# A two-layer hybrid decoder trunk: one more Strassen-Winograd step in each gate/up group, with block sums and raw weights in four shared slots

## The chip, the cores and the metric

The kernel runs on one core of a Trainium2 chip. The metric is the device time of one execution in microseconds (us). PE is the matrix engine (PEld its weight loads), DVE the vector engine, ACT the scalar engine, POOL the GpSimd engine and SP the engine whose queue issues the weight loads. Each engine works through its own list of instructions, fixed when the program is built; semaphores order the engines among each other.

## The reference

256 tokens of width 2048 pass through two layers, in float32. Layer 0 mixes tokens by trailing means over 2, 4, 8 and 16 tokens and a 512x512 product per channel group; layer 1 by differential attention with 8 heads. A SwiGLU network with 5632 hidden columns stands behind each mixer.

```python
def swiglu(h, wg, wu, wd):
    return (jax.nn.silu(h @ wg) * (h @ wu)) @ wd

for i in range(DEPTH):                       # DEPTH = 2
    hn = rmsnorm(h, norm_mix[i])
    mix = pool_mixer(...) if i == 0 else diff_attention(...)
    h = h + mix
    h = h + swiglu(rmsnorm(h, norm_ffn[i]), w_gate[i], w_up[i], w_down[i])
return rmsnorm(h, final_norm)
```

## The kernel before, in words

**Float32 through three products.** Every operand is kept as two parts of the matrix engine's 32-bit format: a rounded `hi` and the rest `lo`. A product is hi·hi + hi·lo + lo·hi, three matmuls of 128x128 by 128x512. For the weights this means, for each 1 MB tile `raw` of 128x(4x512) that SP's queue loads: ACT casts it to `whi` (line 115), and DVE subtracts, `wlo = raw - whi` (line 116).

**Groups and steps.** `group` computes four 128x512 results (two token blocks by two column blocks) as a sum over eight steps, one for each pair of input chunks (six steps in the down products of the last chunk). In the network of a layer, a gate/up group holds the gate columns on the left and the up columns on the right; there are eleven, in `CHUNKS` of 4, 4 and 3, and each chunk is followed by two down products (`o` = 0, 1) that read the chunk's hidden tiles `h`.

**Two kinds of step.** A plain step makes eight block products, 24 matmuls, and needs whi and wlo of all four blocks of `raw` (128x2048). A step "by sevens" multiplies the 2x2 blocks in the Strassen-Winograd way: seven products, 21 matmuls. For that DVE first forms four block sums `tsum` of the raw weights (`sums`: one instruction of 128x1024 in line 121, two of 128x512 in lines 123 and 124), ACT casts them to `thi` (line 130) and DVE forms `tlo = tsum - thi` (line 131); of the raw blocks only three are needed in halves (128x1536). `SEVEN` lists the steps of a gate/up group that go by sevens, `SEVEN_DOWN` those of a down product. `tsum`, `thi` and `tlo` have one buffer each, `raw`, `whi` and `wlo` three each.

**The end of a group.** `combined` (lines 195 to 212) turns the seven accumulators, each in a PSUM bank of its own, and the plain steps' results into the four results: two copies on ACT and eight additions on DVE (lines 202 to 211). Behind a gate/up group come silu on ACT (line 463), the product with up on DVE (line 464), and `pair`: transposes on PE into PSUM, and the halves of the hidden tile, with the block differences where the down step goes by sevens (lines 247 to 268).

**What sets the order.** A scheduler lists the instructions of each engine when the program is built; each engine keeps to its list on the chip. SP's queue issues the loads in order, each when its `raw` buffer is free.

Of the kernel before, what the change touches and what calls it, by code (L numbers as in the profile page):

```python
# [9 lines left out]
F32 = mybir.dt.float32  # L10
F32R = mybir.dt.float32r
AF = mybir.ActivationFunctionType
ALU = mybir.AluOpType
# [25 lines left out]

SEVEN = (2, 4, 6)  # L40
SEVEN_DOWN = (2, 4, 6)
# [11 lines left out]
def trunk_kernel(ctx, tc, x_n, gains, scale_in, final_in, subln, lam_in, band, dist,  # L53
# [21 lines left out]
    def bank(i, shape=(P, 512)):  # L75
        return psum.tile(list(shape), F32, name=f"b{i}", tag=f"b{i}")


    def aux(shape=(P, 512)):
# [5 lines left out]
    dist_sb = const.tile([P, 2 * P], F32, name="dist_sb")  # L85
    ident = const.tile([P, P], F32, name="ident")
    ones = const.tile([P, P], F32, name="ones")
    nc.vector.memset(ones, 1.0)
    make_identity(nc, ident)

    x_tok = resid.tile([P, 2, D], F32, name="x_tok")
# [26 lines left out]

    def sums(pool, raw):
        t = pool.tile([P, 4, 512], F32, name="tsum")  # L120
        nc.vector.tensor_tensor(t[:, T1:T3 + 1], raw[:, B11:B22 + 1],  # L121
                                raw[:, B12:B12 + 1].broadcast_to([P, 2, 512]), ALU.add)
        nc.vector.tensor_tensor(t[:, T2], t[:, T1], raw[:, B22], ALU.add)  # L123
        nc.vector.tensor_tensor(t[:, T4], t[:, T2], raw[:, B21], ALU.add)  # L124
        return t
# [12 lines left out]
    def group(steps, pool, by_bank=0):  # L138


        plan = []
        for a, seven, src in steps:
            if seven:
                plan.append([(M1, [(A11, 0, B11)]), (M2, [(A12, 0, B21)]), (M6, [(S2, 1, T2)]), (M7, [(S3, 1, T3)]),
                             (P5, [(S1, 1, T1)]), (P3, [(S4, 0, B22)]), (P4, [(A22, 1, T4)])])
            else:
                plan.append([(C11, [((0, 0), 0, B11), ((1, 0), 0, B21)]), (C12, [((0, 0), 0, B12), ((1, 0), 0, B22)]),
                             (C21, [((0, 1), 0, B11), ((1, 1), 0, B21)]), (C22, [((0, 1), 0, B12), ((1, 1), 0, B22)])])
        left = {}
# [3 lines left out]
        ps = {}  # L153

        def prepared(seven, src):
            raw = load(src)
            t = sums(pool, raw) if seven else None
            w = [halves(raw, B11 if seven else 0)]
            if seven:
                w.append(sum_halves(pool, t))  # L160
            return w

        def products(a, seven, w, b, parts):
            first = b not in ps
            if first:
                ps[b] = bank(b)
            for at, which, block in parts:
                hi, lo = w[which]
                if seven:
                    ah, al = a[:, 0, at], a[:, 1, at]  # L170
                else:
                    k, t = at
                    if a.shape[2] == 8:
                        slot = ((A11, A21), (A12, A22))[k][t]
                        ah, al = a[:, 0, slot], a[:, 1, slot]
                    else:
                        ah, al = (a[:, k, i, t * P:(t + 1) * P] for i in range(2))
                for x, y in ((ah, hi), (ah, lo), (al, hi)):
                    left[b] -= 1
                    nc.tensor.matmul(ps[b], x, y[:, block], start=first, stop=(left[b] == 0))  # L180
# [12 lines left out]
        return ps  # L193

    def combined(ps, pool):


        if M1 not in ps:
            return [[ps[C11], ps[C12]], [ps[C21], ps[C22]]]
        m1, u2, u3, p5 = (pool.tile([P, 512], F32, name=f"c{i}") for i in ("11", "12", "21", "22"))  # L200
# [6 lines left out]
        nc.vector.tensor_tensor(p5, p5, u3, ALU.subtract)  # L207
        nc.vector.tensor_tensor(u2, ps[P3], u2, ALU.add)
# [35 lines left out]

    def pair(dst, src, gains, seven):

        ps = aux((P, 2, 2, P))
        for i in range(2):
# [31 lines left out]
    with tc.tile_pool(name="start", bufs=1, reuse_waits="tile") as st:  # L280

        warm = tmp.tile([P, 8], F32, name="warm", bufs=1)
        nc.scalar.activation(warm[:, 0:1], ones[:, 0:1], AF.Sqrt)
# [4 lines left out]
        w_pool = [st.tile([P, 4, 512], F32, name=f"w{g}") for g in range(PLAIN)]  # L288
        scale_sb = st.tile([P, D], F32, name="scale_sb")
# [17 lines left out]
        load_x(1)  # L307
        nc.sync.dma_start(out=w_pool[1], in_=pool_w[1])
        w_pool.append(load(pool_w[2]))
# [22 lines left out]
        def product(g, some):  # L332

            if some[0] == 0:
                yp[g] = [bank(4 + 2 * (g % 2) + t) for t in range(2)]
                if g >= PLAIN:
                    w_pool[g] = halves(w_pool[g])
# [75 lines left out]
    turn["of"] = 4  # L413
    nc.sync.dma_start(out=dist_sb, in_=dist)

    def finish(cs, ys, final_sb, ss):

        for t in range(2):
            part = tmp.tile([P, 64], F32, name="part", bufs=2)
            nc.vector.tensor_reduce(part[:, 0:1], ss[:, t, 0:2], AX.X, ALU.add)  # L420
# [22 lines left out]
    def ffn(layer, xq, ss, next_op, next_gain):  # L443
# [3 lines left out]
        with tc.tile_pool(name=f"ffn{layer}", bufs=1, reuse_waits="tile") as hp:  # L447
            g0 = 0
            ys = []
            for c, n in enumerate(CHUNKS):  # L450
# [6 lines left out]
                for g in range(g0, g0 + n):  # L457

                    by_seven = SEVEN[-1:] if g == 0 and layer == 0 else SEVEN
                    cs = combined(group([(xq[p], p in by_seven, w_gu[layer][g, p]) for p in range(NP)], hp), hp)  # L460
# [4 lines left out]
                    for i in range(2):  # L465
                        at = 2 * (g - g0) + i
                        ht = hp.tile(pair_shape(at in SEVEN_DOWN), F32R, name="h", tag=f"h{at}")
                        pair(ht, lambda k, t: cs[t][1][:, (2 * i + k) * P:(2 * i + k + 1) * P], None, at in SEVEN_DOWN)
                        hp_tiles.append(ht)
                for o in range(2):  # L470
# [13 lines left out]
                    for b, t in ((0, 0), (0, 1), (1, 0), (1, 1)):  # L484
# [5 lines left out]
                        if last and next_op is None:  # L490
                            if b == 0 and t == 0:
                                ys.append([hp.tile([P, 2, 2, 512], F32, name="y", tag=("tsum", "thi")[i]) for i in range(2)])
                                ys = ys[0]
# [12 lines left out]
    with tc.tile_pool(name="attn", bufs=1, reuse_waits="tile") as ap_, ExitStack() as heads:  # L506
# [86 lines left out]
        for g in range(2):  # L593
            cs = scaled(combined(group([(xp[p], p in SEVEN_QKV, w_v[g, p]) for p in range(NP)], op_), op_), (r_col, r_col))
            for h in range(4 * g, 4 * g + 4):
# [11 lines left out]
                for t in range(2):  # L607
                    nc.scalar.activation(on[:, t, :], op[:, t, :], AF.Copy, scale=ro[:, t:t + 1])
                oT[h] = op_.tile(pair_shape(h in SEVEN_O), F32R, name=f"oT{h}")
                pair(oT[h], lambda i, t: on[:, t, i * P:(i + 1) * P], [gs[:, i:i + 1] for i in range(2)], h in SEVEN_O)  # L610
# [98 lines left out]
```

## Time and profile before

| | us |
|---|---|
| median of the runs | 1845.46 (1845.2 to 1845.46) |
| profiled execution, its own time | 1846.21 |
| its span, first to last instruction | 1844.4 |
| PE busy | 1829.2 (99%) |
| PEld busy | 1495.6 (81%) |
| DVE busy | 1604.2 (87%) |
| ACT busy | 1038.0 (56%) |
| granted PE clock | 0.997 |

An engine is busy from the start to the end of an instruction, and instructions of one engine overlap at their edges, so the step from start to start is shorter than the duration of one. PE's matmuls overlap far more: one lasts 392 ns by its row, and the next starts about 227 ns after it.

### The profile page before, as it was taken

How to read it: one execution, taken by the hardware profiler on the slowest of the kernel's cores; microseconds unless marked ns; L12 is line 12 of the kernel's file. 1: busy time of each engine (PE TensorE's matmuls, PEld its weight loads, DVE VectorE, ACT ScalarE, POOL GpSimd, SP SyncE). 2: the span in 40 equal slices, each digit the busy share in tenths (PEclk: the TensorE clock that was granted, in tenths of full speed). 3: DMA queues.
4: the chain of work that ended last, by engine and by line, in shares of the span. 5: the costliest groups of instructions: out<-in, count | busy, mean ns of one | idle time of the engine just before them, and what ended most of it. 6: DMA issues, size and time to landing. Idle time of an engine off the chain costs nothing.

```text
span 1844.4 us, 20901 instructions
## 1 busy us (share of the span) xinstructions
PE 1829.2 (99%) x8210; PEld 1495.6 (81%) x8210; DVE 1604.2 (87%) x1662; ACT 1038.0 (56%) x1006; POOL 0.7 (0%) x6
## 2 busy tenths in 40 slices
PE   9999999999999999999999999999999999999998
PEld 6788888888888888888888888788888888888886
DVE  6889998898989899988888678998989899998986
ACT  6555555555554556665566655555555555545553
POOL 0000000000000000000000000000000000000000
PEclk9999999999999999999999999999999999999999
DMA  7555555655555555555454454555555555565552
GB/s 273 183 201 187 193 210 194 210 196 194 203 198 204 202 186 183 208 180 171 173 177 164 160 188 176 205 203 187 204 205 204 188 201 183 206 227 204 206 186 111
DMA packets 50642, 356.80 MB, mean 193 GB/s; under 512 B 6000, under 2 KB 6128, under 8 KB 8048
## 3 DMA queue, kind: packets, MB, share of 16 engines
q1 hardware_dynamic: 49824, 353.85, 54.4%
q10 hardware_dynamic: 720, 1.62, 0.2%
q8 instruction: 64, 1.05, 0.2%
q14 instruction: 34, 0.28, 0.0%
HBM read 353.36 MB, written 2.10 MB: 193 GB/s over the span
## 4 chain that ended last, share of the span: by engine, by line
PE 95%; DVE 2%; ACT 1%; issue 1%; DMA 1%; SPq 0%; DVEq 0%; ACTq 0%
PE b L180 90%; PE b L250 2%; PE b L342 1%; DVE wlo L116 1%; PE b L554 1%; PE b L345 1%; PE b L584 0%; DMA w<-pool_w 0%; DMA raw<-w_gu 0%; DVE tlo L131 0%; ACT whi L115 0%; DVE tsum L121 0%; PE b L600 0%; PE b L598 0%; PE b L599 0%
## 5 line engine op out<-in xcount | busy, mean ns | idle before, releaser
L115 ACT CAST whi<-raw 128x1536 fp32r<-128x1536 f32 (+1 forms) x330 | 585.2, 1774 | 585.4 <-PE b L180 499.6
L180 PE MATMUL b<-whi,xp 128*128 128x512 f32 x2824 | 908.8, 392 | 1.2 <-DVE c L203 1.0
L116 DVE TENSOR_TENSOR wlo<-raw,whi 128x1536 fp32r<-128x1536 f32 (+1 forms) x330 | 697.3, 2113 | 193.1 <-ACT whi L115 192.9
L180 PEld LDWEIGHTS b<-whi,xp 128*128 128x128 f32 x2824 | 528.3, 188 | 110.1 <-DVE c L203 1.5
L180 PE MATMUL b<-wlo,xp 128*128 128x512 f32 x1412 | 551.8, 391 | 1.6 <-DVE wlo L116 1.6
L180 PE MATMUL b<-whi,h 128*128 128x512 f32 x1108 | 354.5, 390 | 0.0
L180 PEld LDWEIGHTS b<-wlo,xp 128*128 128x128 f32 x1412 | 265.3, 188 | 55.5 <-DVE wlo L116 1.9
L131 DVE TENSOR_TENSOR tlo<-tsum,thi 128x2048 fp32r<-128x2048 f32 x108 | 246.7, 2285 | 3.9 <-ACT thi L130 3.9
L180 PEld LDWEIGHTS b<-whi,h 128*128 128x128 f32 x1108 | 207.5, 188 | 43.1
L180 PE MATMUL b<-wlo,h 128*128 128x512 f32 x554 | 215.8, 389 | 0.0
L130 ACT CAST thi<-tsum 128x2048 fp32r<-128x2048 f32 x108 | 206.3, 1910 | 13.7 <-DVE tsum L124 13.6
L180 PE MATMUL b<-thi,xp 128*128 128x512 f32 x608 | 211.8, 390 | 0.0
L121 DVE TENSOR_TENSOR tsum<-raw 128x1024 f32<-128x1024 f32 x108 | 131.8, 1220 | 2.3 <-DMA raw<-w_v 0.6
L180 PEld LDWEIGHTS b<-thi,xp 128*128 128x128 f32 x608 | 113.9, 188 | 24.0 <-ACT thi L130 0.9
L180 PEld LDWEIGHTS b<-wlo,h 128*128 128x128 f32 x554 | 104.0, 188 | 21.3
L180 PE MATMUL b<-tlo,xp 128*128 128x512 f32 x304 | 119.5, 393 | 0.0
L180 PE MATMUL b<-thi,h 128*128 128x512 f32 x240 | 83.7, 389 | 0.0
L124 DVE TENSOR_TENSOR tsum<-tsum,raw 128x512 f32<-128x512 f32 x108 | 74.3, 688 | 2.3
L123 DVE TENSOR_TENSOR tsum<-tsum,raw 128x512 f32<-128x512 f32 x108 | 73.9, 684 | 0.6
L180 PE MATMUL b<-whi,oT 128*128 128x512 f32 x236 | 74.4, 392 | 0.0
L180 PEld LDWEIGHTS b<-tlo,xp 128*128 128x128 f32 x304 | 57.0, 188 | 16.1 <-DVE tlo L131 4.4
L180 PEld LDWEIGHTS b<-thi,h 128*128 128x128 f32 x240 | 45.1, 188 | 9.2
(147 smaller groups left out, 1192.5 us busy)
## 6 DMA issues: line engine op xcount, KB each, us to landing
raw<-w_gu SPq DMA_DIRECT2D x176, 1024.0 KB, 4.9
raw<-w_down SPq DMA_DIRECT2D x88, 1024.0 KB, 4.8
raw<-w_qk SPq DMA_DIRECT2D x32, 1024.0 KB, 4.9
raw<-w_v SPq DMA_DIRECT2D x16, 1024.0 KB, 4.8
raw<-w_o SPq DMA_DIRECT2D x16, 1024.0 KB, 4.8
raw<-pool_w SPq DMA_DIRECT2D x2, 1024.0 KB, 13.8
x_tok<-x_n SPq DMA_DIRECT2D x2, 768.0 KB, 9.0
w<-pool_w SPq DMA_DIRECT2D x2, 512.0 KB, 6.6
```

Source lines behind the costliest of these rows:

```text
L115: nc.scalar.copy(hi[:, lo_block:], raw[:, lo_block:])
L116: nc.vector.tensor_tensor(lo[:, lo_block:], raw[:, lo_block:], f32(hi[:, lo_block:]), ALU.subtract)
L121: nc.vector.tensor_tensor(t[:, T1:T3 + 1], raw[:, B11:B22 + 1], raw[:, B12:B12 + 1].broadcast_to([P, 2, 512]), ALU.add)
L123: nc.vector.tensor_tensor(t[:, T2], t[:, T1], raw[:, B22], ALU.add)
L124: nc.vector.tensor_tensor(t[:, T4], t[:, T2], raw[:, B21], ALU.add)
L130: nc.scalar.copy(hi, t)
L131: nc.vector.tensor_tensor(lo, t, f32(hi), ALU.subtract)
L180: nc.tensor.matmul(ps[b], x, y[:, block], start=first, stop=(left[b] == 0))
L250: nc.tensor.transpose(ps[:, i, 1 - t if seven else t], src(i, t), ident)
L342: nc.tensor.matmul(yp[g][t], a[:, rows], w[:, at], start=(at == 0), stop=(at == 3))
L345: nc.tensor.matmul(yp[g][t], u, v[:, at], start=(at == 0 and j == 0), stop=(at == 3 and j == 2))
L554: nc.tensor.matmul(sc[:, :nk], qk[:, 0, c, qb * P:(qb + 1) * P], qk[:, 1, c, :nk], start=True, stop=True)
```

## The change

- **`SEVEN` goes from (2, 4, 6) to (0, 2, 4, 6).** The first gate/up group of layer 0 keeps only step 6 by sevens, and that of layer 1 keeps (2, 4, 6); the other ten of each layer have four steps by sevens, and so four plain ones. The attention products and the down products keep their lists.
- **Buffers.** `raw` and `tsum` share one ring of four buffers; before, `raw` had three and `tsum` one of its own. A buffer is handed on in the order of the program, four allocations later.
- **`group`.** The products of a step by sevens are issued in another order: those on raw weights first, those on sums behind. P3 and P4 sit in two neighbouring banks that are allocated together.
- **`combined`.** Two subtractions become one instruction over 2x512 columns, and so do the two additions that read P3 and P4 (lines 211 and 212 of the changed kernel). Six DVE instructions where eight were.
- **`pair` of the hidden tiles** transposes into bank X instead of a rotating one. Small tiles (`ones`, `dist_sb`, `part`, the attention outputs of heads 4 to 7) move to other pools.

```diff
-SEVEN = (2, 4, 6)
+SEVEN = (0, 2, 4, 6)
...
-    wraw = ctx.enter_context(tc.tile_pool(name="wraw", bufs=3))
+    wraw = ctx.enter_context(tc.tile_pool(name="wraw", bufs=4))
...
-        raw = wraw.tile([P, 4, 512], F32, name="raw")
+        raw = wraw.tile([P, 4, 512], F32, name="raw", tag="raw")
...
-        t = pool.tile([P, 4, 512], F32, name="tsum")
+        t = wraw.tile([P, 4, 512], F32, name="tsum", tag="raw")
...
-                plan.append([(M1, [(A11, 0, B11)]), (M2, [(A12, 0, B21)]), (M6, [(S2, 1, T2)]), (M7, [(S3, 1, T3)]),
-                             (P5, [(S1, 1, T1)]), (P3, [(S4, 0, B22)]), (P4, [(A22, 1, T4)])])
+                raw = [(M1, [(A11, 0, B11)]), (M2, [(A12, 0, B21)]), (P3, [(S4, 0, B22)])]
+                summed = [(P5, [(S1, 1, T1)]), (M7, [(S3, 1, T3)]), (M6, [(S2, 1, T2)]), (P4, [(A22, 1, T4)])]
+                late = 3 if plan else 2
+                plan.append(raw[:late] + summed[:3] + raw[late:] + summed[3:])
...
-        nc.vector.tensor_tensor(u2, p5, u2, ALU.subtract)
-        nc.vector.tensor_tensor(p5, p5, u3, ALU.subtract)
-        nc.vector.tensor_tensor(u2, ps[P3], u2, ALU.add)
-        nc.vector.tensor_tensor(u3, ps[P4], u3, ALU.add)
+        nc.vector.tensor_tensor(c[:, 1:4:2], c[:, 3:4].broadcast_to([P, 2, 512]), c[:, 1:3], ALU.subtract)
+        nc.vector.tensor_tensor(c[:, 1:3], ps["both"], c[:, 1:3], ALU.add)
...
-                    by_seven = SEVEN[-1:] if g == 0 and layer == 0 else SEVEN
+                    by_seven = SEVEN if g else SEVEN[1:] if layer else SEVEN[-1:]
...
-                        pair(ht, lambda k, t: cs[t][1][:, (2 * i + k) * P:(2 * i + k + 1) * P], None, at in SEVEN_DOWN)
+                        pair(ht, lambda k, t: cs[t][1][:, (2 * i + k) * P:(2 * i + k + 1) * P], None, at in SEVEN_DOWN, X)
```

DVE in the middle of a gate/up group, before (a step by sevens from its sums to `tlo`, and the plain step's `wlo` between them):

```order
L121 TENSOR_TENSOR tsum<-raw 128x1024
L116 TENSOR_TENSOR wlo<-raw,whi 128x1536
L123 TENSOR_TENSOR tsum<-tsum,raw 128x512
L124 TENSOR_TENSOR tsum<-tsum,raw 128x512
L116 TENSOR_TENSOR wlo<-raw,whi 128x2048
L131 TENSOR_TENSOR tlo<-tsum,thi 128x2048
```

The same place now, for steps 4 and 5 of a group:

```order
L120 TENSOR_TENSOR tsum<-raw 128x1024
L115 TENSOR_TENSOR wlo<-raw,whi 128x1536
L122 TENSOR_TENSOR tsum<-tsum,raw 128x512
L123 TENSOR_TENSOR tsum<-tsum,raw 128x512
L130 TENSOR_TENSOR tlo<-tsum,thi 128x2048
L115 TENSOR_TENSOR wlo<-raw,whi 128x2048
```

The plain step's `wlo` (128x2048) stood between the last sum and `tlo`; now it stands behind `tlo`, and nothing stands between. So it is at 28 places in each layer's network from its first combination to that of its eleventh group; before at none of them.

DVE at the end of a gate/up group, before (lines 202 to 211 are the combination, 464 the product with up; 116 belongs to the next group's plain first steps and 121, 123 to its step 2):

```order
L202 TENSOR_TENSOR c_9573<-b_9394,c_9572 128x512
L121 TENSOR_TENSOR tsum<-raw 128x1024
L204 TENSOR_TENSOR c_9574<-b_9398,c_9573 128x512
L203 TENSOR_TENSOR c_9572<-b_9315,c_9572 128x512
L206 TENSOR_TENSOR c_9573<-c_9575,c_9573 128x512
L116 TENSOR_TENSOR wlo<-raw,whi 128x2048
L207 TENSOR_TENSOR c_9575<-c_9575,c_9574 128x512
L208 TENSOR_TENSOR c_9573<-b_9322,c_9573 128x512
L209 TENSOR_TENSOR c_9574<-b_9329,c_9574 128x512
L211 TENSOR_TENSOR c_9575<-b_9336,c_9575 128x512
L464 SCALAR_TENSOR_TENSOR c_9573<-c_9573,r_tok,c_9572 128x512
L464 SCALAR_TENSOR_TENSOR c_9575<-c_9575,r_tok,c_9574 128x512
```

And now (120, 122, 123 are sums of the next group's step 0, 115 and 130 its `wlo` and `tlo`):

```order
L122 TENSOR_TENSOR tsum<-tsum,raw 128x512
L211 TENSOR_TENSOR c<-c 128x2x512
L123 TENSOR_TENSOR tsum<-tsum,raw 128x512
L212 TENSOR_TENSOR c<-b_2880,c 128x1024
L214 TENSOR_TENSOR c<-b_2911,c 128x512
L470 SCALAR_TENSOR_TENSOR c<-c,r_tok 128x512
L115 TENSOR_TENSOR wlo<-raw,whi 128x1536
L470 SCALAR_TENSOR_TENSOR c<-c,r_tok 128x512
L130 TENSOR_TENSOR tlo<-tsum,thi 128x2048
```

The next group's first step needed one `wlo`, which stood ahead of the combination's end; now it needs three sums, `wlo` and `tlo`, and both halves stand behind the combination's last addition.

PE at that boundary, before (b_9618 to b_9632 are the next group's banks, line 250 the transposes of the hidden tile):

```order
L180 MATMUL b_9618<-whi,xp 128x512
L180 MATMUL b_9618<-wlo,xp 128x512
L180 MATMUL b_9618<-whi,xp 128x512 x2
L180 MATMUL b_9618<-wlo,xp 128x512
L180 MATMUL b_9618<-whi,xp 128x512
L180 MATMUL b_9625<-whi,xp 128x512
```

And now:

```order
L184 MATMUL b_3166<-whi,xp 128x512
L184 MATMUL b_3182<-whi,xp 128x512
L184 MATMUL b_3170<-thi,xp 128x512
L184 MATMUL b_3174<-thi,xp 128x512
L184 MATMUL b_3178<-thi,xp 128x512
L253 MATMUL b_3127<-ident,c 128x128
L184 MATMUL b_3162<-wlo,xp 128x512
```

Where eighteen matmuls on whole products ran first, five matmuls on hi parts now stand ahead of the transposes and of the first that needs `wlo`.

More of the change, by code (lines that the diff above doesn't have):

```diff
@@ L76, in bank, with two_banks @@
         return psum.tile(list(shape), F32, name=f"b{i}", tag=f"b{i}")
+    def two_banks():
+        both = psum.tile([P, 2, 512], F32, name="b45", tag="b45")
+        return [both[:, i] for i in range(2)], both
     def aux(shape=(P, 512)):
@@ L117, in halves, with sums @@
         return hi, lo
-    def sums(pool, raw):
-        t = pool.tile([P, 4, 512], F32, name="tsum")
+    def sums(raw):
+        t = wraw.tile([P, 4, 512], F32, name="tsum", tag="raw")
         nc.vector.tensor_tensor(t[:, T1:T3 + 1], raw[:, B11:B22 + 1],
@@ L152, in group @@
                 left[b] = left.get(b, 0) + 3 * len(parts)
-        ps = {}
+        ps, opened = {}, set()
         def prepared(seven, src):
             raw = load(src)
-            t = sums(pool, raw) if seven else None
+            t = sums(raw) if seven else None
             w = [halves(raw, B11 if seven else 0)]
@@ L163, in products @@
         def products(a, seven, w, b, parts):
-            first = b not in ps
-            if first:
+            first = b not in opened
+            opened.add(b)
+            if first and b in (P3, P4) and b not in ps:
+                (ps[P3], ps[P4]), ps["both"] = two_banks()
+            elif first and b not in ps:
                 ps[b] = bank(b)
@@ L199, in combined @@
             return [[ps[C11], ps[C12]], [ps[C21], ps[C22]]]
-        m1, u2, u3, p5 = (pool.tile([P, 512], F32, name=f"c{i}") for i in ("11", "12", "21", "22"))
+        c = pool.tile([P, 4, 512], F32, name="c")
+        m1, u2, u3, p5 = (c[:, i] for i in range(4))
         nc.scalar.copy(m1, ps[M1])
@@ L243, in split, with pair @@
         nc.vector.scalar_tensor_tensor(dst[:, 1, :], src, gain, f32(dst[:, 0, :]), ALU.mult, ALU.subtract)
-    def pair(dst, src, gains, seven):
-        ps = aux((P, 2, 2, P))
+    def pair(dst, src, gains, seven, at=None):
+        ps = aux((P, 2, 2, P)) if at is None else bank(at, (P, 2, 2, P))
         for i in range(2):
@@ L280, in trunk_kernel @@
     with tc.tile_pool(name="start", bufs=1, reuse_waits="tile") as st:
+        ones = st.tile([P, P], F32, name="ones")
+        nc.vector.memset(ones, 1.0)
         warm = tmp.tile([P, 8], F32, name="warm", bufs=1)
+        make_identity(nc, ident)
         nc.scalar.activation(warm[:, 0:1], ones[:, 0:1], AF.Sqrt)
@@ L286, in trunk_kernel @@
             nc.tensor.matmul(wp[:, 0:P], ones, ones, start=True, stop=True)
-        w_pool = [st.tile([P, 4, 512], F32, name=f"w{g}") for g in range(PLAIN)]
+        w_pool = [st.tile([P, 4, 512], F32, name="w0")]
         scale_sb = st.tile([P, D], F32, name="scale_sb")
@@ L307, in trunk_kernel @@
         load_x(1)
-        nc.sync.dma_start(out=w_pool[1], in_=pool_w[1])
+        w_pool.append(load(pool_w[1]))
         w_pool.append(load(pool_w[2]))
@@ L334, in product @@
             if some[0] == 0:
-                yp[g] = [bank(4 + 2 * (g % 2) + t) for t in range(2)]
+                yp[g] = [bank(6 + t) for t in range(2)] if g % 2 else two_banks()[0]
                 if g >= PLAIN:
@@ L413, in trunk_kernel @@
     turn["of"] = 4
-    nc.sync.dma_start(out=dist_sb, in_=dist)
     def finish(cs, ys, final_sb, ss):
         for t in range(2):
-            part = tmp.tile([P, 64], F32, name="part", bufs=2)
+            part = tmp.tile([P, 8], F32, name="warm", bufs=1) if t == 0 else \
+                tmp.tile([P, 2, 4], F32, name="ss").rearrange("p a b -> p (a b)")
             nc.vector.tensor_reduce(part[:, 0:1], ss[:, t, 0:2], AX.X, ALU.add)
@@ L491, in ffn @@
                             if b == 0 and t == 0:
-                                ys.append([hp.tile([P, 2, 2, 512], F32, name="y", tag=("tsum", "thi")[i]) for i in range(2)])
+                                ys.append([hp.tile([P, 2, 2, 512], F32, name="y", tag=("tlo", "thi")[i]) for i in range(2)])
                                 ys = ys[0]
@@ L511, in trunk_kernel @@
             small[:, a:b] for a, b in ((0, 2), (2, 4), (4, 8), (8, 10), (10, 12), (12, 13), (14, 16)))
+        dist_sb = hq.tile([P, 2 * P], F32, name="dist_sb")
+        nc.sync.dma_start(out=dist_sb, in_=dist)
         nc.sync.dma_start(out=subln_sb, in_=subln)
@@ L515, in trunk_kernel @@
         nc.vector.tensor_scalar(qs_col, r_col, QK_SCALE, None, ALU.mult)
+        ones = hq.tile([P, P], F32, name="ones")
+        nc.vector.memset(ones, 1.0)
         nc.vector.tensor_tensor(lp, lam_sb[:, 0:2], lam_sb[:, 2:4], ALU.mult)
@@ L608, in trunk_kernel @@
                     nc.scalar.activation(on[:, t, :], op[:, t, :], AF.Copy, scale=ro[:, t:t + 1])
-                oT[h] = op_.tile(pair_shape(h in SEVEN_O), F32R, name=f"oT{h}")
+                if h < 4:
+                    oT[h] = op_.tile(pair_shape(h in SEVEN_O), F32R, name=f"oT{h}")
+                else:
+                    oT[h] = resid.tile(pair_shape(h in SEVEN_O), F32R, name="xp", tag=f"xp{h}")
                 pair(oT[h], lambda i, t: on[:, t, i * P:(i + 1) * P], [gs[:, i:i + 1] for i in range(2)], h in SEVEN_O)
```

4 lines of the change are left out of this document (removed).

## The prediction

> **What bounds the kernel now.** I read the page's busy times first, then the chain that ended last, then a table of stages, then the vector engine's instructions one by one.
>
> ```profile
> PE 1829.2 (99%) x8210; PEld 1495.6 (81%) x8210; DVE 1604.2 (87%) x1662; ACT 1038.0 (56%) x1006; POOL 0.7 (0%) x6
> ...
> PE b L180 90%; PE b L250 2%; PE b L342 1%; DVE wlo L116 1%; PE b L554 1%; PE b L345 1%; PE b L584 0%; DMA w<-pool_w 0%; DMA raw<-w_gu 0%; DVE tlo L131 0%; ACT whi L115 0%; DVE tsum L121 0%; PE b L600 0%; PE b L598 0%; PE b L599 0%
> ...
> 478.66 124.35 PE b L180 x547
> ```
>
> PE carries the time: the chain is line 180's matmuls to 90%, and a stretch of 547 of them takes 124.35 us, 0.2273 us each. But DVE at 87% is a close second. Stages tell how close. The first two rows go from the first combination of a layer's network to that of its eleventh gate/up group (ten gate/up groups and four down products); the third is one gate/up group, the fourth one down product.
>
> ```profile
> core 0: us, PE busy (x) PEld busy (x) DVE busy (x) ACT busy (x) POOL busy (x), PEclk, DMA share, GB/s
> 86.49:678.77 592.28, 592.27 (x2644) 487.69 (x2643) 535.32 (x471) 322.11 (x238) 0.00 (x0) 1.00 0.56 199
> 1174.54:1764.09 589.55, 588.38 (x2624) 483.86 (x2623) 533.08 (x470) 320.27 (x237) 0.00 (x0) 1.00 0.57 200
> ...
> 128.87:171.59 42.72, 42.72 (x193) 35.01 (x192) 38.86 (x36) 24.16 (x20) 0.00 (x0) 1.00 0.55 197
> 257.04:298.52 41.48, 41.48 (x185) 34.36 (x184) 37.56 (x33) 20.64 (x14) 0.00 (x0) 1.00 0.57 203
> ```
>
> In a gate/up group PE has no gap, and DVE is busy 38.86 of 42.72 us: its room is 3.86 us a group. That room is what the change has to live on.
>
> **The change, part by part.**
>
> *Matmuls removed.* Twenty groups lose three matmuls each: 60 x 0.2273 = 13.6 us of PE. A gate/up group's PE work goes from 42.72 to 42.04 us.
>
> *DVE work added.* What one more step by sevens costs is read from starts, since busy spans overlap:
>
> ```profile
> 1274.68 2.28 DVE L131 TENSOR_TENSOR tlo<-tsum,thi 128x2048 fp32r<-128x2048 f32 x1
> 1276.88 1.75 DVE L116 TENSOR_TENSOR wlo<-raw,whi 128x1536 fp32r<-128x1536 f32 x1
> ...
> 1281.14 2.29 DVE L116 TENSOR_TENSOR wlo<-raw,whi 128x2048 fp32r<-128x2048 f32 x1
> 1283.35 2.29 DVE L131 TENSOR_TENSOR tlo<-tsum,thi 128x2048 fp32r<-128x2048 f32 x1
> 1285.67 1.23 DVE L121 TENSOR_TENSOR tsum<-raw 128x1024 f32<-128x1024 f32 x1
> 1286.84 1.76 DVE L116 TENSOR_TENSOR wlo<-raw,whi 128x1536 fp32r<-128x1536 f32 x1
> 1288.52 0.69 DVE L123 TENSOR_TENSOR tsum<-tsum,raw 128x512 f32<-128x512 f32 x1
> 1289.24 0.69 DVE L124 TENSOR_TENSOR tsum<-tsum,raw 128x512 f32<-128x512 f32 x1
> ...
> 1305.41 0.68 DVE L207 TENSOR_TENSOR c<-c,c 128x512 f32<-128x512 f32 x1
> 1306.01 0.68 DVE L208 TENSOR_TENSOR c<-b,c 128x512 f32<-128x512 f32 x1
> ```
>
> From start to start: the wide sum 1.17, wlo of three blocks 1.68, the second sum 0.72, the third 0.60 (as the 512-column rows of line 207 to 208), tlo 2.20 (1274.68 to 1276.88); the plain step's wlo that falls away 2.21. Together +4.16 us a group. The merged instructions have no row; the nearest is the wide sum, 1.17 against 2 x 0.60, so two merges save 0.06; bounds are nothing and 0.15 each, half a microsecond a group at most either way. I take +4.1, and DVE's busy time in a gate/up group becomes 38.86 + 4.1 = 42.96 us: over PE's new 42.04, and over the old 42.72, before it waits once.
>
> (The Trainium skill, "VectorE: DVE Perf Modes", section "The DRAIN you can't avoid", says that a DVE operation does not start until the pipe of the one before is empty. Read so, each instruction would cost its full duration and a group some 0.2 us more, an estimate of 4 us over 20 groups; here a 2.29 us row is followed by the next start after 2.21, so the starts are used.)
>
> *The wait that the new order makes.* tlo needs thi, which ACT casts from all four sums. Before, the plain step's wlo stood between the last sum and tlo and covered the cast. Now nothing does, 28 times in each layer's stretch. One such place exists in the trace of before:
>
> ```profile
> 738.13 0.69 DVE L124 TENSOR_TENSOR tsum<-tsum,raw 128x512 f32<-128x512 f32 x1
> 740.87 2.29 DVE L131 TENSOR_TENSOR tlo<-tsum,thi 128x2048 fp32r<-128x2048 f32 x1 [2.05 <-ACT thi L130]
> 743.42 2.29 DVE L116 TENSOR_TENSOR wlo<-raw,whi 128x2048 fp32r<-128x2048 f32 x1 [0.26 <-ACT whi L115]
> ...
> L130 ACT CAST thi<-tsum 128x2048 fp32r<-128x2048 f32 x108 | 206.3, 1910 | 13.7 <-DVE tsum L124 13.6
> ```
>
> DVE idles 2.05 us, the cast's 1.91 and two hand-overs. Behind it wait the plain step's wlo and the next step's sums, and PE for both. An in-order engine that bounds the stage cannot win this back. It costs nothing only where DVE has a lead on PE, and in a gate/up group it has none left. I take 2.05 each; the lower bound is 0, were DVE ahead everywhere, the upper 2.3 with the 0.26 of the last row but one.
>
> *The sum.* A gate/up group like the third row needs on DVE 42.96 + 2 x 2.05 = 47.1 us, 4.4 more than before. Groups behind plain pairs have three such waits, a down product one: 37.56 + 2.05 = 39.6, still under its 41.48 of PE.
> Layer 0's stretch: 535.3 + 10 x 4.1 + 28 x 2.05 = 633.7. The order puts 5.3 us of it (1.17 + 0.72 + 0.60 + 1.68 + 1.17) ahead of the stretch. At the end of a chunk's second down product DVE waits for PE, 41.48 - 39.6 = 1.9 us, twice: 3.8. That makes 632.2, against 592.3: +39.9.
> Layer 1's: 533.1 + 41 + 57.4 - 2.9 (one wide sum and one wlo ahead) + 3.8 = 632.4, against 589.6: +42.8.
> Outside the stretches the steps keep their numbers, and PE is the bound there; moved tiles, the extra block differences of one more operand tile (about 1 us of DVE a layer) and the later load of the distances lie beside matmuls. I book 0, with 3 us either way.
> Sum: 1846.2 + 82.7 = 1928.9 on the profiled execution, whose time is 0.75 us over the median of the runs: 1928.
>
> *What else is moved, at no cost.* PE's order at a group's start has five matmuls, 1.1 us, before it needs the new group's wlo, so PE stands there; that is DVE's lateness showing, and not a second term. Bank X for the transposes makes PE wait for ACT's copies, again inside that time. ACT gains a cast of 1.91 and loses a quarter of another: 24.16 becomes about 25.7 of 47.
>
> *Loads.* With the ring of four, a plain step's load waits for the tlo of the step by sevens before it, instead of for an older wlo.
>
> ```profile
> raw<-w_gu SPq DMA_DIRECT2D x176, 1024.0 KB, 4.9
> ...
> DMA to landing us min/median/max: 4.7/4.9/6.5
> ```
>
> From that tlo's end DVE spends 1.17 + 1.68 + 0.72 + 0.69 and then ACT's cast 1.9 until ACT turns to the plain step's cast: 6.2 us. A load of 4.9 is there; one of 6.5 is 0.3 late and still inside the 0.4 that tlo leaves (2.29 against a cast of 1.91). No cost.
>
> **The rivals.**
>
> *It gets faster: DVE stays ahead, and PE's 13.6 us come out.* Then 1845.5 - 13.6 = 1832. For it: PE is 99% busy now, and DVE idles 240 us in all. The point from which it decides is DVE's gate/up group at 42.04 or less; 42.96 misses that without any wait. The lead that a chunk's down products could lend, 1.9 us, covers 2 x 0.92 us, two groups of four. 6%.
>
> *The 2.05 us waits are covered somehow and DVE's work alone bounds the groups.* PE then loses 0.92 x 20 = 18.4, less the lead of six chunks (11 us), against 13.6: 1839 to 1851, about 1846, no change. Against it: the order has nothing between sum and tlo. 4%.
>
> *Worse: a plain step's load lands behind another.* Two loads of 4.9 one after the other would land at 9.8, 3.2 us late past the slack worked out above. Once a group that is 20 x 3.2 = 64 more: 1992. For it: the 6.5 in the row above is a load that shared. Against it: SP issues the plain step's load first, and it would have to share. (The Trainium skill, "DMA: Bandwidth & Descriptors", section "Two DMAs through the same engine are not ordered" says that descriptors of one queue start in order. By that the first load keeps its 4.9 us and the sum stays 1928; shared evenly it would be the 1992. No run here shows it.) 6%.
>
> **How the numbers follow.** DVE-bound as summed: 84%, so 1928. Its own uncertainty: the wait lies between 0 and 2.3 and, being a row of this kernel, near 2.05; if a lead hides a third of it (1.4), 56 of them give -36, at 2.3 they give +14; the merges give 20 x 0.3 = 6 either way; the rest 3. All at once that is 1883 to 1951; they will not all err one way, and I take 1890 to 1950. The rivals at 1832, 1846 and 1992 stay outside. Differences under 0.2% (3.7 us) are no change here: faster 0.06 and 0.01 of the second rival, same 0.02 of it, slower the rest, 0.91.
>
> **What would show it.** DVE's busy share in the gate/up groups over 90% with idle time before line 130 of about 2 us, 56 times or so, released by thi; DVE wlo waiting on whi no longer the longest DVE wait; ACT's whi casts waiting far less on PE; PE idle in short pieces, 4 to 5 us a group, released by DVE; the gate/up group near 47 us and the down products near 41.5. If PE is still without gaps, DVE had a lead that I denied it. If tlo's idle time is there and the time is not, PE's slack was larger than its busy row says. If ACT's casts wait on loads, the third rival is on.

## The result and the profile after

The changed kernel takes 1933.99 us in the median of four runs (1928.91 to 1935.1); the kernel before, on the same chip, 1845.33 (1845.13 to 1845.46). The ratio is 1.0475, 95% interval 1.0457 to 1.0494: 88.7 us slower. The forecast was 1928.

The page of the changed kernel (span 1931.8 us): busy times, chain by engine, and from the groups of instructions the subtraction `tlo` and the two merged instructions of `combined` (busy us, mean ns of one, idle time before them and its releaser).

```profile
PE 1857.4 (96%) x8150; PEld 1483.7 (77%) x8150; DVE 1674.7 (87%) x1665; ACT 1049.9 (54%) x1028; POOL 0.7 (0%) x6
...
PE 54%; DVE 31%; issue 7%; ACT 6%; DMA 1%; SPq 0%; ACTq 0%; DVEq 0%
...
L130 DVE TENSOR_TENSOR tlo<-tsum,thi 128x2048 fp32r<-128x2048 f32 x128 | 292.9, 2288 | 123.5 <-ACT thi L129 123.4
...
L211 DVE TENSOR_TENSOR c<-c 128x1024 f32<-128x1024 f32 x41 | 50.0, 1219 | 0.6
L212 DVE TENSOR_TENSOR c<-b,c 128x1024 f32<-128x1024 f32 x41 | 49.9, 1218 | 0.7 <-PE b L184 0.2
```

PE has 60 matmuls fewer and is no longer the chain: it ran through PE matmuls almost alone before, now DVE and ACT hold 37% of it (`issue` is time for which the profile shows no wait, `q` marks an engine's instruction sequencer). DVE's share of 87% is unchanged, because the span grew with its work; such an average does not show the new bound.

The table of stages, the same stretches as in the prediction, then two gate/up groups and a down product. Columns: the window, its length, busy time (instructions) of PE, PEld, DVE, ACT and POOL, the granted PE clock, the DMA share, GB/s.

```profile
86.53:720.92 634.39, 607.75 (x2615) 483.23 (x2613) 566.26 (x477) 328.31 (x246) 0.00 (x0) 0.99 0.51 185
1214.15:1849.19 635.04, 608.07 (x2618) 482.07 (x2616) 568.67 (x480) 329.85 (x247) 0.00 (x0) 0.99 0.52 187
399.66:446.43 46.77, 43.52 (x190) 34.10 (x189) 42.56 (x39) 24.97 (x20) 0.00 (x0) 1.00 0.49 180
446.43:493.49 47.06, 44.70 (x190) 35.30 (x188) 42.65 (x39) 25.38 (x20) 0.00 (x0) 0.96 0.56 201
538.23:580.01 41.78, 41.78 (x186) 34.58 (x185) 37.84 (x33) 18.82 (x13) 0.00 (x0) 1.00 0.51 184
```

The stretches take 42.1 and 45.5 us more than before, 87.6 together; the time outside them is 662.4 us against 662.6. A gate/up group takes 47 us with DVE busy 42.6: that is the group's bound, plus two waits.

DVE inside one group (start, duration, line, in brackets the idle time before it and its releaser), and ACT in the same stretch:

```profile
475.65 0.69 DVE L123 TENSOR_TENSOR tsum<-tsum,raw 128x512 f32<-128x512 f32 x1
478.39 2.29 DVE L130 TENSOR_TENSOR tlo<-tsum,thi 128x2048 fp32r<-128x2048 f32 x1 [2.05 <-ACT thi L129]
480.61 2.28 DVE L115 TENSOR_TENSOR wlo<-raw,whi 128x2048 fp32r<-128x2048 f32 x1
...
486.33 0.69 DVE L123 TENSOR_TENSOR tsum<-tsum,raw 128x512 f32<-128x512 f32 x1
489.07 2.29 DVE L130 TENSOR_TENSOR tlo<-tsum,thi 128x2048 fp32r<-128x2048 f32 x1 [2.05 <-ACT thi L129]
```

```profile
476.45 1.91 ACT L129 CAST thi<-tsum 128x2048 fp32r<-128x2048 f32 x1 [5.26 <-DVE tsum L123]
478.27 3.28 ACT L114 CAST whi<-raw 128x2048 fp32r<-128x2048 f32 x2
```

From the last sum, ACT casts for 1.91 us while DVE stands; ACT itself had stood 5.26 us for that sum, and 2.05 us of DVE's standing come again 10.7 us later. Two engines take turns, and neither is busy throughout: DVE 42.6 of 47 us, ACT 25. The waits of the whole trace (waiter, releaser: us in total, times, longest us):

```profile
ACT thi L129 <- DVE tsum L123: 388.7, 96, 8.8
ACT whi L114 <- PE b L184: 175.7, 84, 5.5
DVE tlo L130 <- ACT thi L129: 123.4, 65, 2.1
DVE wlo L115 <- ACT whi L114: 85.7, 57, 4.1
...
ACT whi L114 <- DMA raw<-w_gu: 7.8, 8, 1.7
```

### The profile page after: what moved, and what is told of

Its sections match the earlier page's. It is cut to its first block, busy times and chain, and to the rows that moved or that the text cites. A ratio compares the mean times of both kernels' runs of the same rounds, so it can differ in the third digit from the quotient of the medians.

```text
span 1931.8 us, 20620 instructions
## 1 busy us (share of the span) xinstructions
PE 1857.4 (96%) x8150; PEld 1483.7 (77%) x8150; DVE 1674.7 (87%) x1665; ACT 1049.9 (54%) x1028; POOL 0.7 (0%) x6
## 4 chain that ended last, share of the span: by engine, by line
PE 54%; DVE 31%; issue 7%; ACT 6%; DMA 1%; SPq 0%; ACTq 0%; DVEq 0%
PE b L184 50%; DVE wlo L115 13%; ACT thi L129 4%; DVE tsum L120 3%; DVE tlo L130 3%; DVE tsum L122 2%; DVE c L212 2%; DVE tsum L123 2%; ACT whi L114 2%; DVE c L211 1%; PE b L253 1%; DVE c L208 1%; DVE c L209 1%; PE b L564 1%; DMA raw<-w_down 1%
## 5 line engine op out<-in xcount | busy, mean ns | idle before, releaser
L115 DVE TENSOR_TENSOR wlo<-raw,whi 128x1536 fp32r<-128x1536 f32 (+1 forms) x330 | 685.8, 2079 | 86.0 <-ACT whi L114 85.7
L114 ACT CAST whi<-raw 128x1536 fp32r<-128x1536 f32 (+1 forms) x330 | 570.3, 1742 | 229.6 <-PE b L184 175.7
L184 PEld LDWEIGHTS b<-whi,xp 128*128 128x128 f32 x2732 | 512.6, 189 | 138.5 <-DVE c L212 19.4
L129 ACT CAST thi<-tsum 128x2048 fp32r<-128x2048 f32 x128 | 244.5, 1910 | 393.7 <-DVE tsum L123 388.7
L130 DVE TENSOR_TENSOR tlo<-tsum,thi 128x2048 fp32r<-128x2048 f32 x128 | 292.9, 2288 | 123.5 <-ACT thi L129 123.4
L184 PE MATMUL b<-thi,xp 128*128 128x512 f32 x784 | 265.2, 396 | 8.3 <-ACT thi L129 8.2
L184 PEld LDWEIGHTS b<-thi,xp 128*128 128x128 f32 x784 | 146.4, 189 | 44.2 <-ACT thi L129 15.7
L184 PE MATMUL b<-tlo,xp 128*128 128x512 f32 x392 | 156.5, 399 | 7.6 <-DVE tlo L130 7.6
L120 DVE TENSOR_TENSOR tsum<-raw 128x1024 f32<-128x1024 f32 x128 | 155.9, 1218 | 2.6 <-DMA raw<-w_v 2.1
L184 PEld LDWEIGHTS b<-tlo,xp 128*128 128x128 f32 x392 | 74.0, 189 | 32.4 <-DVE tlo L130 18.6
L123 DVE TENSOR_TENSOR tsum<-tsum,raw 128x512 f32<-128x512 f32 x128 | 88.1, 688 | 2.6
L122 DVE TENSOR_TENSOR tsum<-tsum,raw 128x512 f32<-128x512 f32 x128 | 87.5, 684 | 0.2
L469 ACT ACTIVATE c<-c,r_tok 128x512 f32<-128x512 f32 x44 | 31.8, 724 | 69.1 <-DVE c L208 49.2
```

The costliest lines, as they stand in the source:

```text
L114: nc.scalar.copy(hi[:, lo_block:], raw[:, lo_block:])
L115: nc.vector.tensor_tensor(lo[:, lo_block:], raw[:, lo_block:], f32(hi[:, lo_block:]), ALU.subtract)
L129: nc.scalar.copy(hi, t)
L130: nc.vector.tensor_tensor(lo, t, f32(hi), ALU.subtract)
L469: nc.scalar.activation(gate, gate, AF.Silu, scale=r[:, t:t + 1])
```

## The experiments

Two theories stood. **A, a serial chain:** the ring of four puts the plain step's cast and `wlo` behind the sums of the step by sevens, and DVE and ACT then wait for one another; without that chain nearly all of the loss is gone. **B, work:** DVE's added instructions alone are over what a group allows, and the waits are only where the lack of time shows.

### The wait on the cast taken away

`tlo` no longer reads `thi`, so it need not wait for it; `other` is `t` itself, and the low parts of the sums are left out of the result.

```diff
-    def sum_halves(pool, t):
+    def sum_halves(pool, t, other):
...
-        nc.vector.tensor_tensor(lo, t, f32(hi), ALU.subtract)
+        nc.vector.tensor_tensor(lo, t, f32(other), ALU.subtract)
```

> The changed kernel, but tlo = tsum - tsum instead of tsum - thi: the same instruction on the same engine in nearly the same order, which no longer waits for ACT's cast (the low parts of the sums are left out of the result). Theory (DVE is the bound by its work and by 56 uncovered casts of 2.05 us): only the work is left, 42.6 to 43.0 us on DVE for a gate/up group against 42.04 on PE, so each layer's stretch falls from 634 to 586 to 598, and the time from 1934 to 1838 to 1860. Rival 1 (the added DVE work alone makes the loss, the waits are slack): no change, 1925 to 1934. Rival 2 (loads of the shared ring come late): the wait moves from the cast to the loads, over 1900.

Measured: 1914.42 us (1913.87 to 1914.97), ratio 1.0372 (1.0351 to 1.0393). Only 20 us came back; the theory's 1838 to 1860 missed. DVE and ACT of this kernel at the same place of a group, then its wait of `wlo`:

```profile
484.14 0.69 DVE L123 TENSOR_TENSOR tsum<-tsum,raw 128x512 f32<-128x512 f32 x1
484.93 2.29 DVE L130 TENSOR_TENSOR tlo<-tsum 128x2048 fp32r<-128x2048 f32 x1
488.70 4.59 DVE L115 TENSOR_TENSOR wlo<-raw,whi 128x2048 fp32r<-128x2048 f32 x2 [1.47 <-ACT whi L114]
```

```profile
484.94 1.92 ACT L129 CAST thi<-tsum 128x2048 fp32r<-128x2048 f32 x1 [5.19 <-DVE tsum L123]
486.76 1.90 ACT L114 CAST whi<-raw 128x2048 fp32r<-128x2048 f32 x1
```

```profile
DVE wlo L115 <- ACT whi L114: 173.3, 116, 4.1
```

The wait moved by one instruction. ACT's list has the plain tile's cast right behind the sums' cast, so `wlo` now waits 1.47 us for it. From the last sum to `wlo` it is 4.56 us (484.14 to 488.70), against 4.96 in the changed kernel (475.65 to 480.61). The cast at 486.76 waits for no load: it is its place in the list that makes it late. Over the whole trace DVE's waits for the two casts fall only from 209.1 us (123.4 and 85.7) to 173.3.

### The sums in a buffer of their own

```diff
-    wraw = ctx.enter_context(tc.tile_pool(name="wraw", bufs=4))
+    wraw = ctx.enter_context(tc.tile_pool(name="wraw", bufs=3))
...
-        t = wraw.tile([P, 4, 512], F32, name="tsum", tag="raw")
+        t = wraw.tile([P, 4, 512], F32, name="tsum", tag="tsum", bufs=1)
```

> The changed kernel with the buffers of before: raw three, tsum one of its own. The order then has tlo directly behind the last sum at 34 places of the two stretches instead of 56. Theory: 22 x 2.05 = 45 us come back, 1934 - 45 = 1889 (1875 to 1900). Rival 1 (DVE work alone): no change, 1925 to 1934. Rival 2 (the shared ring is the whole loss): all of it comes back, 1832 to 1850.

Measured: 1937.36 us (1933.85 to 1940.87), ratio 1.0496 (1.0474 to 1.0519), no better than the change. The expectation failed. The waits of this kernel:

```profile
DVE wlo L115 <- ACT whi L114: 118.4, 91, 4.2
DVE tlo L130 <- ACT thi L129: 90.1, 56, 3.1
ACT whi L114 <- DMA raw<-w_gu: 71.2, 52, 3.0
```

The wait of `tlo` fell from 123.4 to 90.1 us, that of `wlo` rose from 85.7 to 118.4: DVE waits as long as before. With three raw buffers the casts wait 71.2 us for `w_gu` where they waited 7.8; that these loads are the reason is not shown. The split of the buffers only trades one wait for another, so it is not the sharing of the ring alone that makes the loss.

### Everything but the fourth seven

```diff
-SEVEN = (0, 2, 4, 6)
+SEVEN = (2, 4, 6)
```

The first gate/up group of layer 0 keeps its one step by sevens, every other group has three.

> The changed kernel with SEVEN back at (2, 4, 6), as before the change; the shared ring, the merges, the bank and the new order stay. The order has 22 uncovered casts in the two stretches. Theory: a gate/up group needs 38.8 + 2.05 = 40.9 us of DVE and 42.7 of PE, so PE bounds again and the waits cost nothing: 1845 (1842 to 1850). Rival 1 (DVE work alone): the same 1845. Rival 2 (the shared ring delays loads): slower than before by 10 us or more.

Measured: 1843.33 us (1841.36 to 1844.43), ratio 0.9986 (0.9977 to 0.9995). The shared ring, the new order of products and the merged instructions cost nothing by themselves; with three sevens `tlo` still waits 58.2 us in all (36 times), and PE does not notice, because a group leaves DVE room. So the 90.7 us between this and the complete change belong to the fourth seven in that setting.

### Two of the sums on POOL

```diff
-        nc.vector.tensor_tensor(t[:, T2], t[:, T1], raw[:, B22], ALU.add)
-        nc.vector.tensor_tensor(t[:, T4], t[:, T2], raw[:, B21], ALU.add)
+        nc.gpsimd.tensor_tensor(t[:, T2], t[:, T1], raw[:, B22], ALU.add)
+        nc.gpsimd.tensor_tensor(t[:, T4], t[:, T2], raw[:, B21], ALU.add)
```

> The changed kernel with the two 128x512 additions of each set of sums on POOL instead of DVE. DVE's gate/up group loses 4 x (0.72 + 0.60) = 5.3 us and falls to 37.7, and no tlo stands directly behind a sum of DVE. No row of this kernel shows an addition on POOL: it stays hidden up to 42 / 8 = 5.2 us each. Theory: PE bounds again, with its 60 matmuls less: 1845.3 - 13.6 = 1832 (1830 to 1840). Rival 1 (DVE work alone): the same 1832. Rival 2 (loads late): over 1900. A further way: DVE runs slower while POOL works beside it, 1850 or more.

Measured: 2055.4 us, ratio 1.1136 (1.1117 to 1.1154). This took work off DVE, 128 x 2 additions of 0.69 us, and put it into the chain. POOL's groups of this kernel, and its waits:

```profile
L122 POOL TENSOR_TENSOR tsum<-tsum,raw 128x512 f32<-128x512 f32 x128 | 300.2, 2345 | 1493.9 <-DVE tsum L120 1019.0 <-issue 245.5 <-DVE e L268 65.4
L123 POOL TENSOR_TENSOR tsum<-tsum,raw 128x512 f32<-128x512 f32 x128 | 190.4, 1488 | 10.0
```

```profile
ACT thi L129 <- POOL tsum L123: 591.9, 110, 10.8
DVE tlo L130 <- ACT thi L129: 330.0, 112, 4.5
```

The two additions take 3.8 us in a row instead of 1.4 (mean rows; spans on POOL are rough), and the chain is longer by that: `tlo` waits 330 us instead of 123.4. DVE had less to do and the kernel lost 121 us more. B alone cannot give that; a longer chain can. The theory's 1832 missed all the same, and so did the first rival's; the theory had taken POOL's additions as hidden. What DVE's slower instructions beside POOL (last section) add to the loss was not measured apart.

### The next tile loaded before the sums

The complete change, and one thing moved: in `group` the tile of the next step is taken from the ring and its load issued ahead of the sums of the present step. Then a plain step's load no longer waits in the ring for the `tlo` of an earlier step by sevens (of step 0 for the load of step 3, and so on).

```diff
+        raw = load(steps[0][2])
-        for (a, seven, src), step in zip(steps[:head], plan[:head]):
-            w = prepared(seven, src)
+        for n, ((a, seven, src), step) in enumerate(zip(steps[:head], plan[:head])):
+            ahead = load(steps[n + 1][2]) if n + 1 < head else None
+            w = prepared(seven, raw)
+            raw = ahead
```

> The changed kernel, complete, but each step's raw tile is taken from the ring before the sums of the step ahead of it. In the ring of four a plain step's load then waits for a raw tile that is read early, no longer for the tlo of the last step by sevens. The order has the plain step's cast and wlo between the last sum and tlo nearly everywhere; 24 uncovered casts are left in the two stretches, 20 of them singly in groups. Theory as it stands after the first runs (the loss is a serial chain of DVE's sums, ACT's two casts one behind the other and DVE's two subtractions, because the plain step's load arrives after the sums): the chain goes, DVE's work of 42.6 to 43.0 us against 42.0 of PE bounds the groups, with 2.05 us where a cast is still uncovered: 1836 to 1862. Rival 1 (the added work on DVE alone is the loss, in whatever order): 1915 to 1934. Rival 2 (the ring itself delays loads): over 1900, with waits on loads.

Measured: 1848.26 us (1846.08 to 1849.28), ratio 1.0011 (1.0001 to 1.0020). This order of the loads alone brings back 86 of the 89 us. Its wait of `tlo`, DVE at the sums of one step, and from the stage table a gate/up group and the whole stretch of layer 0:

```profile
DVE tlo L130 <- ACT thi L129: 30.2, 31, 2.1
```

```profile
443.44 0.68 DVE L123 TENSOR_TENSOR tsum<-tsum,raw 128x512 f32<-128x512 f32 x1
444.04 3.95 DVE L115 TENSOR_TENSOR wlo<-raw,whi 128x2048 fp32r<-128x2048 f32 x2
447.91 2.28 DVE L130 TENSOR_TENSOR tlo<-tsum,thi 128x2048 fp32r<-128x2048 f32 x1
```

```profile
425.87:469.22 43.35, 42.36 (x189) 34.23 (x188) 42.04 (x38) 25.95 (x21) 0.00 (x0) 1.00 0.58 209
```

```profile
89.51:680.17 590.66, 587.83 (x2607) 479.47 (x2606) 567.50 (x478) 333.90 (x247) 0.00 (x0) 1.00 0.56 199
```

Two `wlo` lie between the last sum and `tlo` again, and cover the cast. This group takes 43.35 us where the change took 47, with the same work on DVE: in the stretch DVE is busy 567.5 us, against 566.3 in the changed kernel, and its waits for `thi` and `whi` fall from 64.2 to 18.8 us. So the chain cost 86 us. What stays looks like B: with 30 matmuls (6.8 us) fewer the stretch takes 590.66 us against 592.28 before. DVE is busy 96% of it, where it was 90%, and PE is idle for 2.8 us. DVE's work then costs what the matmuls give; that it is the work, and not the waits that are left, is argued and not shown by a run of its own.

### Three matmuls put back

One block product counted twice in each of the 20 groups, so PE has its 60 matmuls again.

```diff
+                if not plan:
+                    raw[0][1].append(raw[0][1][0])
```

> The changed kernel with three matmuls more in the first step of each of the 20 groups by four sevens, so that PE has as many as before the change (one block product is counted twice in the result). Theory (DVE and ACT bound the groups, PE waits 4 to 5 us in each): nothing, 1930 to 1938. Rival (PE is still on the path that sets the end): 60 x 0.227 = 13.6 us more, 1948.

Measured: 1931.61 us (1930.22 to 1932.99), ratio 1.0464 (1.0443 to 1.0485), the time of the change. In the changed kernel 13.6 us of matmuls are worth nothing.

### The fourth seven in every other group

In the odd groups alone (ten in all), with the early load, with the change's order, and as a control the early load with three sevens everywhere.

```diff
-                    by_seven = SEVEN if g else SEVEN[1:] if layer else SEVEN[-1:]
+                    by_seven = SEVEN if g % 2 else SEVEN[1:] if g or layer else SEVEN[-1:]
```

> The order of loads of e5, and the fourth seven only in the odd gate/up groups: 5 groups a layer, 10 in all, in place of 20. Theory (the serial chain is gone with the early load, what stays is DVE's work): a group with four sevens asks 42.6 to 43.0 us of DVE against 42.0 of TensorE, and the next group, with three, leaves DVE 3.9 us of room, so the 30 matmuls that go (6.8 us) are kept: 1843.3 - 6.8 = 1836.5, 1833 to 1841. Rival (DVE does not carry its lag over a group's end, since the cast tiles are too few): each of the ten loses what the others of e5 lose, about 0.7 us, on top of e5's order: 1843 to 1848.

> The fourth seven only in the odd gate/up groups, the order of loads as in the change. Theory (the loss comes from the serial chain of the group with four sevens, group by group): half of the change's 90.7 us over e3 stays: 1888, 1878 to 1896. Rival (the loss builds up because groups with four sevens follow one another, and a group with three between them gives it back): 1840 to 1860.

> Three sevens in every gate/up group, with the order of loads of e5. Theory: TensorE bounds these groups, so the early load changes nothing against e3's 1843.3: 1841 to 1846, and e7's gain is the matmuls'. Rival (the early load is worth something of its own, or costs something by a raw tile held longer): 1833 to 1840 or over 1848.

Measured: 1842.28 us (1841.14 to 1843.15), ratio 0.9980 (0.9971 to 0.9989); without the early load 1874.01, ratio 1.0150 (1.0134 to 1.0165); the control 1848.49, ratio 1.0012 (1.0003 to 1.0021). Two windows of the first of the three, by first combinations. DVE works ahead of PE: in the first window it forms four sets of sums, in the second three, and PE multiplies the group with four sevens in the second.

```profile
382.39:426.98 44.59, 44.59 (x202) 36.70 (x201) 43.00 (x38) 25.52 (x22) 0.00 (x0) 1.00 0.52 186
426.98:467.72 40.74, 40.74 (x183) 33.00 (x182) 38.46 (x35) 23.70 (x20) 0.00 (x0) 1.00 0.52 193
```

PE is busy throughout both, and they take 85.3 us together: DVE's 43.0 and 38.5 fit. The time, 1842.28, lies between the theory's range and its rival's; but against the control, which has the same order of loads, the 30 matmuls bring 6.2 us (30 x 0.2273 is 6.8), as the theory had it. Where in the groups they come out is not shown. The control itself is 5.2 us slower than the third experiment (their intervals are apart): its theory's 1841 to 1846 missed, and its rival's "over 1848" came. The window from the second down product's first combination to that of the next gate/up group, in the control and in the third experiment:

```profile
299.89:341.79 41.90, 41.90 (x185) 34.19 (x184) 37.25 (x31) 20.54 (x15) 0.00 (x0) 1.00 0.56 200
```

```profile
297.94:339.41 41.47, 41.47 (x185) 34.34 (x184) 37.17 (x31) 20.32 (x15) 0.00 (x0) 1.00 0.56 203
```

The early load makes each of the eight windows that begin with a down product's first combination 0.4 us longer (those between the two down products and those behind them), 3.3 of the 5.2 us; 0.9 lie ahead of the first combination (at 87.98 us instead of 87.07). Without it, half of the groups keep a third of the loss, 30.7 of 90.7 us: a group with three sevens behind one with four gives some back. 1874 lies between A's 1878 to 1896 and the rival's 1840 to 1860; both missed.

### The early load in gate/up groups alone

Two ways to save those 0.4 us: the early load in all gate/up groups, or in the odd ones only, and nowhere else; the fourth seven stays in the odd groups.

```diff
-            ahead = load(steps[n + 1][2]) if n + 1 < head else None
+            ahead = load(steps[n + 1][2]) if early and n + 1 < head else None
```

> e7 with the early load in the gate/up groups alone; down products and attention load as in the change. In the trace of e9 the early load makes each down product 41.9 us instead of 41.5 (TensorE's weight load waits up to 0.4 us for tlo there), and the start 0.9 us later. Theory: 10 down products x 0.42 = 4.2 us come back and the ten groups with four sevens keep their 6 us: 1838, 1835 to 1841. Rival (the early load costs wherever it stands, or its cost moves to the group that follows): 1841 to 1844, as e3 and e7.

> The early load only in the ten groups with four sevens, and the change's order everywhere else. Theory: as e10, since the groups with three sevens don't need it: 1838, 1835 to 1841. Rival (a group that begins with the early load after one without it finds the ring in another turn and pays a wait at its start): over 1842.

Measured: 1850.5 us, ratio 1.0024 (1.0015 to 1.0034), and 1847.57, ratio 1.0011 (1.0002 to 1.0020). Both theories missed; the second one's rival had "over 1842". The first one's window between the first combinations of the two down products behind an early group:

```profile
511.62:555.04 43.42, 43.34 (x189) 34.74 (x187) 37.24 (x31) 19.98 (x14) 0.00 (x0) 1.00 0.54 194
```

It is 43.4 us instead of 41.9, though DVE is busy 37 us of it: with a change of order between groups the kernel loses more than the 0.4 us that were to be saved. Whether a turn of the ring does it stays open. Of all versions the odd groups with the early load, 1842.28, and the third experiment, 1843.33, are under the kernel before; the intervals of their ratios overlap, so neither is shown to be the better.

## Why the prediction was right

*The wait.* 28 waits of 2.05 us in each stretch were forecast, 57.4 us. DVE's waits in layer 0's stretch and in layer 1's:

```profile
DVE tlo L130 <- ACT thi L129: 57.5, 28, 2.1
...
DVE tlo L130 <- ACT thi L129: 58.6, 29, 2.1
```

One uncovered place in the old trace had the price of all. What the prediction read too narrowly is the cause: it gave the time to the one wait, and the first experiment shows that without it the next cast in ACT's list holds DVE for nearly as long. The size was right because `wlo` behind `tlo` hid that second cast.

*DVE's work.* By the prediction's terms DVE would be busy 571 us in each stretch without its waits; it was 566.3 and 568.7, so the added work was 0.3 to 0.5 us a group too dear. The merged instructions measure 1219 and 1218 ns, as the wide sum that stood for them.

*The stretches.* 632.2 and 632.4 were forecast, 634.4 and 635.0 measured. DVE's idle time in layer 0's is 68.1 us: 57.5 at `tlo`, 6.7 at `wlo`, and 3.9 in small pieces. The forecast had 57.4 and 3.8, and only the 57.4 is borne out: its 3.8 was to be DVE waiting for PE at the end of the down products, and DVE waits 0.2 us for PE in this stretch. So the sum is closer than its terms, and that much is luck: in layer 0 the work was put 4.7 us too high and the 3.8 did not come, and 6.7 us at `wlo` and 3.9 in small pieces, which the sum did not have, make up for them. The shares inside a chunk were off: groups of 46.8 and 47.1 came out as forecast, but the two windows that end with a down product's first combination take 43.3 to 44.7 and 41.8 to 42.2 us (42.7 and 41.5 before), and that of the gate/up group behind them 44.8 to 44.9 (41.5 before).

*Outside the stretches* 0 was booked, and it is -0.2. *Matmuls*: the sum had no gain from them, and the experiment that puts them back agrees. *PE's idle time* was given as 4 to 5 us a group; it is 3.3 and 2.4 in the two groups above, since part of the delay lies in longer matmul rows: PE is busy 607.75 us of layer 0's stretch, 592.27 before, with fewer matmuls. The forecast's other marks hold: `wlo` on `whi` is no longer DVE's longest wait, and ACT's casts wait 175.7 us on PE instead of 499.6.

*Loads* were booked at no cost: the casts' 7.8 us of waiting for `w_gu` bear that out, and the rival of loads behind one another is off. The margin was thinner than reckoned: the 6.5 us are the slowest load of a short piece of the old trace, and over its two stretches the slowest take 7.2 and 7.6. In the changed kernel the casts also wait 34.5 us for `w_down`; what that costs is not shown. But the order of the loads has its cost all the same, through the place of the cast in ACT's list. The prediction took the order as given and priced it; that the loads' order makes it is the experiments' finding.

*The rival at 1846*, "the waits are covered and DVE's work alone bounds the groups", gave 1839 to 1851. With the early load just that case was built, and measured 1848.26. *The rival at 1832* needs DVE's group at 42.04; with 42.0 to 43.0 the gain was not had with four sevens in all groups, and it was, but for 0.6 us, with four in every other group.

*What the sum lacked:* 2.2 and 2.6 us in the two stretches. On DVE's side they are the remainder of the terms above. The sum also took the granted clock as constant, and the falls shown below lie in these stretches; how much of the 4.8 us is theirs stays open.

## What to carry to other kernels

When a change moves work to an engine that is second in the table, take its busy time per stage, not per span, and then look in its list for what stands between a hand-over to another engine and the way back: nothing there means the other engine's full time, once per turn, if the waiting engine has no room left (with three sevens 58.2 us of such waits cost nothing). The turn at which a tile is taken from a ring sets that order without a word in the code, so an earlier allocation can be worth more than any arithmetic (86 us here), while a buffer of their own for the sums brought nothing. And taking one wait out of a chain of turns moves it to the next; make the instructions between lie in another order instead.

## What the hardware showed

**The clock can fall where PE is starved by pieces.** In 6 of the 176 windows of 10 us between 90 and 1850 us the granted clock of the changed kernel is under 0.9; in the kernel before and in the version with the early load, in none of 171. PE's rows at the start of a gate/up group, then 4 us there and the 4 us behind them, and the same two windows at the start of another group:

```profile
631.42 0.50 PE L184 MATMUL b<-whi,xp 128*128 128x512 f32 x1 [1.02 <-DVE c L212]
...
634.93 0.63 PE L184 MATMUL b<-whi,xp 128*128 128x512 f32 x1
635.36 0.63 PE L184 MATMUL b<-wlo,xp 128*128 128x512 f32 x1
```

```profile
630.34:634.34 4.00, 1.64 (x6) 0.81 (x5) 4.00 (x5) 4.00 (x3) 0.00 (x0) 0.88 0.03 14
634.34:638.34 4.00, 4.00 (x11) 3.23 (x12) 3.86 (x4) 2.28 (x3) 0.00 (x0) 0.50 0.11 14
...
405.12:409.12 4.00, 1.62 (x6) 0.81 (x5) 4.00 (x5) 4.00 (x3) 0.00 (x0) 1.00 0.00 0
409.12:413.12 4.00, 3.99 (x21) 3.24 (x22) 4.00 (x4) 2.84 (x5) 0.00 (x0) 1.00 0.11 14
```

At the first place no idle piece is longer than 1.02 us, but PE is busy 1.64 of 4 us, and then the clock is 0.50 and matmuls step by 0.43 us (634.93 to 635.36) instead of 0.23. At the second PE is busy as little, and the clock stays at 1.00. Of thirteen group starts in this trace with PE busy under 1.7 of 4 us, the clock fell behind seven; what decides is not shown. The group of the first place took 49.28 us and its twin in the other chunk of the layer 47.63. (The Trainium skill, "TensorE: Matmul & The Clock Gate", section "HAM oscillation — how this bites in real kernels", warns of idle gaps over about 3.4 us; here the clock fell with no piece longer than a third of that. The section "A second HAM failure mode: psum-queue depth-cycling" tells of short idle pieces that do it, and these falls agree with that one.) What all the falls cost was not measured by itself.

**POOL and DVE hold each other up.** DVE in the kernel with sums on POOL, and POOL there:

```profile
475.03 1.75 DVE L115 TENSOR_TENSOR wlo<-raw,whi 128x1536 fp32r<-128x1536 f32 x1
476.70 0.68 DVE L207 TENSOR_TENSOR c<-b,c 128x512 f32<-128x512 f32 x1
...
478.21 2.17 DVE L211 TENSOR_TENSOR c<-c 128x1024 f32<-128x1024 f32 x1
```

```profile
475.33 2.60 POOL L122 TENSOR_TENSOR tsum<-tsum,raw 128x512 f32<-128x512 f32 x1 [7.82 <-DVE tsum L120]
478.01 1.29 POOL L123 TENSOR_TENSOR tsum<-tsum,raw 128x512 f32<-128x512 f32 x1
```

Line 211, which reads two operands from SBUF, takes 2.17 us beside POOL's addition instead of 1.22; line 207, with one operand in PSUM, keeps its 0.68 beside the first one; and POOL's own addition is 2.60 us in one place and 1.29 in the other. In these rows the instruction that starts second is the one that takes longer: POOL's first addition, begun during line 115, and then line 211, begun during POOL's second. Over this trace line 211 takes 1.22 us on average where no addition of POOL runs beside it (22 times) and 2.08 where one does (19 times). (The Trainium skill, "GPSIMD Engine Reference", section "1. Specifications", has POOL's access to SBUF shared with VectorE and names contention with instructions of two SBUF inputs; these rows agree.) Moving work to an idle engine slowed instructions of the busy one.
